# Depthwise convolution: the running sum kept in a PSUM bank instead of SBUF

## The chip, the core and the metric

The kernel runs on one core of a Trainium2 chip. The metric is the device time of one execution in microseconds (us), the median of several runs. A core has a matmul engine (PE, with its own weight-load queue PEld), a vector engine (DVE), an activation engine (ACT), a general engine (POOL), DMA queues (SP issues most of them), the on-chip memory SBUF and the accumulator memory PSUM in eight banks, one of which holds 128 partitions of 512 float32 numbers. Each engine works through its instructions in program order; an instruction that waits holds back all that stand behind it on its engine.

## What is computed

Two transformer blocks follow each other on 512 tokens of width 1024. The change lies in the first one, whose first half is this (cut):

```python
h = rmsnorm(x, norm1_g)
z = h @ w_in                                # conv_in 2048, q 1024, k 256, v 256, two gates of 1024
u = conv_in[..., :1024] * sigmoid(conv_in[..., 1024:])
u = depthwise_conv(u, dw_w, kernel=31, padding=15) + dw_b      # each of 1024 channels by itself
conv_out = silu(layernorm(u)) @ w_pw
attn_out = windowed_gqa(q, k, v, sink) @ w_o                   # 16 heads, window of 128
merged = sigmoid(g0) * conv_out + sigmoid(g1) * attn_out
x = x + merged @ w_out
x = x + peer_ffn(rmsnorm(x))                                   # experts, the long middle part
```

The second block (a recurrence, two attentions, a merge) and the last norm follow.

## The kernel before

Channels lie on the partitions. `u` is a tile of 8 blocks of 128 channels with 542 columns (512 tokens and 15 columns of padding on either side), `acc` one of 8 blocks of 512 columns; both are in SBUF.

The first stage, `mix1_in`, does the following, in the order in which the program writes it. For each of the 8 channel blocks, two projections (`mm_t`) and their product give `u` (the product is POOL's, L439). Then the values `v`. Then a pass of attention (`attn1`) over the first half of the heads and the 8 projections of the first gate; then the second pass, the convolution (`conv`, L524) with the sums for its layer norm (`conv_rms`, L534), and the 8 projections of the second gate. Then the attention's output is split in a high and a low part (`oh` by ACT, L339, `ol` by DVE, L340) and goes through `w_o`; `conv_norm` finishes the convolution; `w_pw` and `w_out` follow.

Every product of float32 matrices is made as three matmuls on their high and low parts (`mm3`, L322 to L324). One `mm_t` is 24 such matmuls into one bank named `ps`, and it needs one slab of weights: a DMA, a copy by ACT (`whi`, L316) and a subtraction of two SBUF tiles on POOL (`wlo`, L317). Slabs have two buffers. A pass of attention first projects the keys (ACT copies them, L575 and L576, DVE makes their low part, L578) and four query blocks (L586, L587), and then goes over four windows: logits (PE, L618), mask and maximum (DVE, L620), exponential (ACT, L627), division (DVE, L634), transposes (PE, L641) that DVE and ACT copy out (L643), and the product with the values (PE, L645).

The convolution of one block is one instruction at L528, `acc = u[0:512] * w[0] + bias`, and 30 at L531, `acc = u[j:j+512] * w[j] + acc`, all on DVE, 248 in all. Each reads what the one before it of the same block wrote, and so waits for it. `conv_rms` sums the eight blocks (L542), takes the mean over channels with a matmul of ones into the bank `pm` (L543), subtracts it from each block (L545), squares (ACT, L547), sums (L549), multiplies by ones again (L550) and makes the reciprocal root (L551, ACT at L1052 and L1053, DVE at L356 to L358).

PSUM has four banks `ps`, three `pa` (attention) and one `pm` in this stage. A scheduler in the build sets the order on each engine from its own estimates, the dependences and the buffers that are free; the program's order is only its starting point. It has put the convolution among the attention's instructions on DVE.

Of the kernel before, what the change touches and what calls it, by code (L numbers as in the profile page):

```python
# [15 lines left out]
OP = mybir.AluOpType  # L16
# [73 lines left out]
def _layout(inp):  # L90
# [5 lines left out]
    hp = _head_perm()  # L96
    hcol = (hp[:, :, None] * 64 + np.arange(64)).reshape(8, 128)
    arr["w1t"] = _tslabs(w, np.concatenate([conv, 2048 + hcol, _blocks(3072, 3328), _blocks(3584, 5632)]))
    arr["w1v"] = _mslabs(w[:, 3328:3584], 256, 4)
    arr["w_pw"] = _tslabs(f["conv_w_pw"][0], _blocks(0, 1024))  # L100
# [139 lines left out]
class Kern:  # L240
# [283 lines left out]
    def conv(self, u, acc):  # L524
        nc, C = self.nc, self.const
        for b in range(8):
            w = C["dw_w"][:, b * 31:(b + 1) * 31]
            nc.vector.tensor_scalar(acc[:, b, :], u[:, b, 0:512], w[:, 0:1], C["dw_b"][:, b:b + 1],  # L528
                                    op0=OP.mult, op1=OP.add)
            for j in range(1, 31):  # L530
                nc.vector.scalar_tensor_tensor(acc[:, b, :], u[:, b, j:j + 512], w[:, j:j + 1], acc[:, b, :],  # L531
                                               op0=OP.mult, op1=OP.add)

    def conv_rms(self, acc, room, kp):  # L534

# [918 lines left out]
```

## Time and profile before

| | us |
|---|---|
| median of three runs | 2652.63 (2636.78, 2652.63, 2659.26) |
| profiled execution | 2650.43 |
| its span | 2648.7 |
| PE busy | 2300.6 (87%) |
| DVE busy | 1839.5 (69%) |
| ACT busy | 838.3 (32%) |
| POOL busy | 738.1 (28%) |
| mean granted TensorE clock | 0.937 |

The span is the stretch from the first to the last instruction in the profile; the time of the execution has 1.7 us more around it. Busy time is an average over very different stages. What the change touches lies in the first 425 us: the convolution's instructions start at 38.4 us and end at 346 us. A row of the trace names the engine, the source line, the operation, and the tiles as output<-inputs.

### The profile page before, as it was taken

The numbers are of one execution on the slowest core, as the hardware profiler recorded it, in microseconds if no ns is written. First come the engines' busy times: TensorE is split into PE (matmuls) and PEld (weight loads), VectorE is DVE, ScalarE is ACT, GpSimd is POOL, SyncE is SP. The second block draws the span as 40 slices with busy tenths as digits, with TensorE's granted clock in tenths as the row PEclk, the third lists the DMA queues.
The fourth block names the chain that finished last, engine by engine and source line by source line (L and its number), as shares of the span: only waits on it lengthen the run. The fifth ranks groups of instructions, "written<-read, shape, count | busy, mean of one in ns | idle before, by whom it ended". The sixth has DMA issues, their size and how long they took to land. (4 is left out here: it accounts for less than half of the span.)

```text
span 2648.7 us, 31665 instructions
## 1 busy us (share of the span) xinstructions
PE 2300.6 (87%) x11682; PEld 1671.9 (63%) x11682; DVE 1839.5 (69%) x3541; ACT 838.3 (32%) x1781; POOL 738.1 (28%) x443
## 2 busy tenths in 40 slices
PE   7938899989989948678867868999789999999999
PEld 6826667868877725445544545663266788768887
DVE  7999975549998867575746656767767666675333
ACT  4214355333236711111111111111153433554321
POOL 4512313223126933343433433434110000000000
PEclk9969999989999979889978989999989999999999
DMA  4201113332457799998989989999731010121323
GB/s 169 96 32 45 59 48 127 120 98 81 171 203 262 256 374 387 404 412 336 415 342 390 410 350 405 408 416 417 323 115 41 25 33 27 56 88 64 104 96 120
DMA packets 142523, 551.16 MB, mean 208 GB/s; under 512 B 12704, under 2 KB 47392, under 8 KB 107040
## 3 DMA queue, kind: packets, MB, share of 16 engines
q1 hardware_dynamic: 105504, 280.69, 29.9%
q0 software_dynamic: 36864, 268.45, 25.1%
q8 instruction: 92, 1.51, 0.2%
q14 instruction: 63, 0.52, 0.1%
HBM read 524.97 MB, written 24.12 MB: 207 GB/s over the span
## 5 line engine op out<-in xcount | busy, mean ns | idle before, releaser
L192 POOL DMA_INDIRECT uv<-uv,ge x256 | 388.8, 1519 | 650.6 <-DVE x L230 576.6
L818 PE MATMUL ps<-hd,u 128*128 128x256 f32 x2048 | 463.5, 381 | 0.0
L818 PEld LDWEIGHTS ps<-hd,u 128*128 128x128 f32 x2048 | 387.1, 192 | 69.9 <-issue 20.0
L230 DVE SCALAR_TENSOR_TENSOR x<-uv,s,x 128x1024 f32<-128x1024 f32 x256 | 328.7, 1284 | 118.7 <-ACT s L222 118.4
L322 PE MATMUL ps<-hh,whi 128*128 128x512 f32 x920 | 370.8, 403 | 42.9 <-ACT whi L316 39.1
L324 PE MATMUL ps<-hh,wlo 128*128 128x512 f32 x920 | 370.9, 403 | 1.2 <-POOL wlo L317 1.2
L323 PE MATMUL ps<-hl,whi 128*128 128x512 f32 x920 | 371.1, 403 | 0.0
L317 POOL TENSOR_TENSOR wlo<-wraw,whi 128x1024 fp32r<-128x1024 f32 x84 | 214.1, 2550 | 505.8 <-ACT whi L316 472.0
L848 PE MATMUL pv<-v,ah 128*128 128x512 f32 x512 | 239.0, 623 | 110.6 <-DMA v<-v 97.1
L219 DVE CUSTOM_DVE_ANT_0 uv<-uv,rows 128x1024 f32<-128x1024 f32 x256 | 317.8, 1241 | 20.5 <-DMA uv<-uv,ge 20.4
L848 PE MATMUL pv<-v,al 128*128 128x512 f32 x512 | 240.9, 622 | 86.3 <-DMA v<-v 65.5
L316 ACT ACTIVATE whi<-wraw 128x1024 fp32r<-128x1024 f32 x151 | 159.8, 1058 | 330.8 <-PE ps L323 239.5
L848 PEld LDWEIGHTS pv<-v,ah 128*128 128x128 f32 x512 | 101.1, 200 | 236.8 <-issue 192.1
L221 ACT ACTIVATE s<-s 128x1 f32<-128x1 f32 x256 | 51.7, 202 | 602.0 <-DVE s L219 601.9
L848 PEld LDWEIGHTS pv<-v,al 128*128 128x128 f32 x512 | 99.7, 199 | 214.7 <-issue 154.1
L322 PEld LDWEIGHTS ps<-hh,whi 128*128 128x128 f32 x920 | 177.0, 192 | 81.3 <-ACT whi L316 39.5
L531 DVE SCALAR_TENSOR_TENSOR acc<-u,cols,acc 128x512 f32<-128x512 f32 x240 | 225.3, 991 | 1.0
L324 PEld LDWEIGHTS ps<-hh,wlo 128*128 128x128 f32 x920 | 176.9, 192 | 39.2 <-issue 2.0
L323 PEld LDWEIGHTS ps<-hl,whi 128*128 128x128 f32 x920 | 176.8, 192 | 39.0 <-issue 4.2
L317 DVE TENSOR_TENSOR wlo<-wraw,whi 128x1024 fp32r<-128x1024 f32 x67 | 81.9, 1223 | 113.2 <-ACT whi L316 112.8
L775 POOL TENSOR_SCALAR B<-colsp,ijw 128x128 f32<-128x128 f32 x64 | 110.9, 1740 | 50.9 <-ACT ijw L764 50.1
L840 DVE TENSOR_TENSOR ah<-ah,cg 128x256 f32<-128x256 f32 x64 | 24.9, 420 | 102.0 <-ACT ah L820 81.9
(489 smaller groups left out, 3403.1 us busy)
## 6 DMA issues: line engine op xcount, KB each, us to landing
u<-u SPq DMA_DIRECT2D x128, 512.0 KB, 8.9
v<-v SPq DMA_DIRECT2D x128, 512.0 KB, 12.5
wraw<-w2t SPq DMA_DIRECT2D x49, 512.0 KB, 3.5
wraw<-w1t SPq DMA_DIRECT2D x42, 512.0 KB, 3.5
gates<-cs SPq DMA_DIRECT2D x16, 1024.0 KB, 7.9
cg<-gates SPq DMA_DIRECT2D x16, 1024.0 KB, 36.0
wraw<-w_out SPq DMA_DIRECT2D x16, 512.0 KB, 3.5
wraw<-w_q SPq DMA_DIRECT2D x16, 512.0 KB, 3.6
```

The source lines that it names most:

```text
L192: self.k.nc.gpsimd.indirect_dma_start(t, None, self.k.ap["uv"], bass.IndirectOffsetOnAxis(ap=self.e[g][:, s:s + 1], axis=0))
L219: nc.vector.tensor_tensor_reduce(out=u, in0=u, in1=self.rows[:, g, :], scale=1.0, scalar=0.0, op0=OP.mult, op1=OP.add, accum_out=d)
L230: self.k.nc.vector.scalar_tensor_tensor(x, t[:, 1024:2048], c, x, op0=OP.mult, op1=OP.add)
L316: nc.scalar.activation(hi, raw, AF.Copy)
L317: (nc.gpsimd if self.low else nc.vector).tensor_tensor(lo, raw, hi.bitcast(F32), op=OP.subtract)
L322: mm(out, ah, bh, start=start, stop=False)
L323: mm(out, ah, bl, start=False, stop=False)
L324: mm(out, al, bh, start=False, stop=stop)
L531: nc.vector.scalar_tensor_tensor(acc[:, b, :], u[:, b, j:j + 512], w[:, j:j + 1], acc[:, b, :], op0=OP.mult, op1=OP.add)
L775: (nc.vector if n < self.near else nc.gpsimd).tensor_scalar(B[:, n, :], C["iota"], ijw[:, 1, t0 + n:t0 + n + 1], ijw[:, 2, t0 + n:t0 + n + 1],
L818: nc.tensor.matmul(ps[:, i * 256:i * 256 + 256], raw[:, k * 128:k * 128 + 128], h[:, k, :], start=k == 0, stop=k == KC - 1)
L848: nc.tensor.matmul(po[t][half], a[:, ts], v[:, half * 512:half * 512 + 512], start=j + i == 0, stop=j + i == 127)
```

## The change

The running sum of each block is kept in a tile `part` of the bank `pm`. The first instruction and those of j = 1 to 29 write there, and the last one, j = 30, reads `part` and writes `acc` in SBUF as before. There is one such bank, so a block's sum can start only when the block before it has ended.

```diff
         for b in range(8):
             w = C["dw_w"][:, b * 31:(b + 1) * 31]
-            nc.vector.tensor_scalar(acc[:, b, :], u[:, b, 0:512], w[:, 0:1], C["dw_b"][:, b:b + 1],
+            part = self.bank("pm")
+            nc.vector.tensor_scalar(part, u[:, b, 0:512], w[:, 0:1], C["dw_b"][:, b:b + 1],
                                     op0=OP.mult, op1=OP.add)
             for j in range(1, 31):
-                nc.vector.scalar_tensor_tensor(acc[:, b, :], u[:, b, j:j + 512], w[:, j:j + 1], acc[:, b, :],
-                                               op0=OP.mult, op1=OP.add)
+                nc.vector.scalar_tensor_tensor(acc[:, b, :] if j == 30 else part, u[:, b, j:j + 512], w[:, j:j + 1],
+                                               part, op0=OP.mult, op1=OP.add)
```

The scheduler answers with another order on DVE, ACT and PE up to the projection `w_o`; behind it every engine's order is as before, and POOL's is the same throughout. In the changed kernel lines behind 527 have numbers higher by one (L531 is L532 there).

On DVE, the start of the convolution before, behind its first L528, up to the first low part of the keys:

```order
L531 SCALAR_TENSOR_TENSOR acc<-u,cols,acc 128x512 x13
L528 TENSOR_SCALAR acc<-u,cols 128x512
L531 SCALAR_TENSOR_TENSOR acc<-u,cols,acc 128x512 x34
L528 TENSOR_SCALAR acc<-u,cols 128x512
L531 SCALAR_TENSOR_TENSOR acc<-u,cols,acc 128x512 x26
L528 TENSOR_SCALAR acc<-u,cols 128x512
L531 SCALAR_TENSOR_TENSOR acc<-u,cols,acc 128x512 x34
L528 TENSOR_SCALAR acc<-u,cols 128x512
L531 SCALAR_TENSOR_TENSOR acc<-u,cols,acc 128x512 x26
L528 TENSOR_SCALAR acc<-u,cols 128x512
L531 SCALAR_TENSOR_TENSOR acc<-u,cols,acc 128x512 x3
L578 TENSOR_TENSOR k<-ps,k 64x512 x2
```

Thirteen instructions belong to block 0 alone; from the second L528 on, two blocks alternate (13 and 34 are the 30 of block 0 and 17 of block 1). In the changed kernel, behind two blocks of 1, 29 and 1 instructions that stand just like the first rows here:

```order
L529 TENSOR_SCALAR pm<-u,cols 128x512
L543 TENSOR_TENSOR u<-acc 128x512
L532 SCALAR_TENSOR_TENSOR pm<-u,cols,pm 128x512 x29
L532 SCALAR_TENSOR_TENSOR acc<-u,cols,pm 128x512
L529 TENSOR_SCALAR pm<-u,cols 128x512
L543 TENSOR_TENSOR u<-u,acc 128x512
L532 SCALAR_TENSOR_TENSOR pm<-u,cols,pm 128x512 x19
L579 TENSOR_TENSOR k<-ps,k 64x512 x2
L532 SCALAR_TENSOR_TENSOR pm<-u,cols,pm 128x512 x2
L579 TENSOR_TENSOR k<-ps,k 64x512 x2
```

The blocks follow each other, and 113 of the 248 instructions stand ahead of the keys instead of 142.

On DVE, the end of the second attention pass before, up to the low part of the attention's output:

```order
L634 TENSOR_SCALAR lg<-lg,s_2388 128x256 x4
L643 COPY pT<-pa 128x512
L340 TENSOR_TENSOR meml<-memT,memh 128x2048
L356 SCALAR_TENSOR_TENSOR u<-pT 128x512
L357 TENSOR_TENSOR u<-u 128x512
L358 SCALAR_TENSOR_TENSOR pT<-u,pT 128x512
L340 TENSOR_TENSOR ol<-o,oh 128x512 x8
```

Now the convolution's last 47 instructions stand among those of this pass, and its last two behind the pass's last copy (L644 now); then come the last L543, four L546, and this:

```order
L550 TENSOR_TENSOR u<-u 128x512
L546 TENSOR_TENSOR acc<-acc,pm 128x512
L550 TENSOR_TENSOR u<-u 128x512 x3
L552 TENSOR_SCALAR u<-pm 128x512
L356 SCALAR_TENSOR_TENSOR u<-pT 128x512
L357 TENSOR_TENSOR u<-u 128x512
L358 SCALAR_TENSOR_TENSOR pT<-u,pT 128x512
L340 TENSOR_TENSOR ol<-o,oh 128x512 x8
```

All of the layer norm's sums have moved from among the attention's windows to behind them, ahead of `ol`.

On PE, the same place before; the rows of the second gate's projection repeat nine times more until `w_o` begins with `oh`:

```order
L645 MATMUL pa<-pT,v 64x512
L641 MATMUL pa<-ident,lg 128x128 x4
L645 MATMUL pa<-pT,v 64x512 x2
L323 MATMUL ps<-hl,whi 128x512
L324 MATMUL ps<-hh,wlo 128x512
L322 MATMUL ps<-hh,whi 128x512
```

And now:

```order
L646 MATMUL pa<-pT,v 64x512
L642 MATMUL pa<-ident,lg 128x128 x4
L646 MATMUL pa<-pT,v 64x512 x2
L544 MATMUL pm<-u,ones 128x512
L551 MATMUL pm<-u,ones 128x512
L323 MATMUL ps<-ol,whi 128x512
L324 MATMUL ps<-oh,wlo 128x512
L322 MATMUL ps<-oh,whi 128x512
```

The gate's projections stand ahead of the last window's end, and behind it PE has nothing but the two matmuls of ones and `w_o`.

## Rows read from the trace of the kernel before

**Rows 1.** By stretch: length, busy PE, PEld, DVE, ACT, POOL (count); clock, DMA share, GB/s.
```profile
38.40:175.70 137.30, 101.79 (x501) 85.72 (x499) 136.78 (x142) 29.21 (x41) 55.76 (x25) 0.88 0.23 77
175.70:204.50 28.80, 19.19 (x62) 14.48 (x62) 28.32 (x31) 9.46 (x13) 9.50 (x4) 0.68 0.20 62
204.50:302.20 97.70, 89.17 (x396) 61.95 (x397) 92.35 (x206) 43.73 (x107) 24.24 (x9) 0.97 0.14 47
302.20:335.60 33.40, 24.64 (x110) 20.27 (x109) 32.56 (x41) 10.18 (x14) 11.92 (x5) 0.93 0.23 79
335.60:421.80 86.20, 83.42 (x365) 55.29 (x365) 65.72 (x163) 53.26 (x123) 17.29 (x8) 0.99 0.15 49
```

**Rows 2.** Busy time by stretch of line L531 alone: length, DVE busy (count), clock, DMA.
```profile
38.40:175.70 137.30, 132.19 (x136) 0.88 0.23 77
204.50:302.20 97.70, 48.74 (x64) 0.97 0.14 47
302.20:335.60 33.40, 19.19 (x15) 0.93 0.23 79
```

**Rows 3.** Timeline of DVE in the convolution: start us, us, engine, line, operation, count.
```profile
43.40 2.33 DVE L531 SCALAR_TENSOR_TENSOR acc<-u,cols,acc 128x512 f32<-128x512 f32 x3
...
51.83 2.77 DVE L531 SCALAR_TENSOR_TENSOR acc<-u,cols,acc 128x512 f32<-128x512 f32 x1
...
155.92 17.31 DVE L531 SCALAR_TENSOR_TENSOR acc<-u,cols,acc 128x512 f32<-128x512 f32 x26
```

**Rows 4.** Timeline of POOL.
```profile
51.28 2.77 POOL L317 TENSOR_TENSOR wlo<-wraw,whi 128x1024 fp32r<-128x1024 f32 x1 [0.82 <-ACT whi L316]
...
179.34 2.35 POOL L317 TENSOR_TENSOR wlo<-wraw,whi 128x1024 fp32r<-128x1024 f32 x1 [46.61 <-ACT whi L316]
```

**Rows 5.** Timeline of ACT where keys and queries begin; brackets: idle before, releaser.
```profile
130.76 0.59 ACT L576 ACTIVATE k<-ps 64x512 fp32r<-64x512 f32 x1
177.12 0.59 ACT L575 ACTIVATE k<-ps 64x512 fp32r<-64x512 f32 x1 [45.77 <-DVE k L578]
...
178.22 1.04 ACT L316 ACTIVATE whi<-wraw 128x1024 fp32r<-128x1024 f32 x1
```

**Rows 6.** Timeline of PE at the same place.
```profile
179.32 0.80 PE L322 MATMUL ps<-hh,whi 128*128 128x512 f32 x1 [39.10 <-ACT whi L316]
```

**Rows 7.** DVE lines one by one: count: nanoseconds min/median/max, first and last start.
```profile
L531 DVE SCALAR_TENSOR_TENSOR acc<-u,cols,acc x240: 711/744/2947, 39.0 to 345.4; 128x512 f32<-128x512 f32 x120
...
L587 DVE SCALAR_TENSOR_TENSOR q<-ps,q x16: 685/689/695, 182.9 to 334.9; 64x512 fp32r<-64x512 f32 x16
...
L545 DVE TENSOR_TENSOR acc<-acc,pm x8: 656/680/686, 348.1 to 364.8; 128x512 f32<-128x512 f32 x8
...
L542 DVE TENSOR_TENSOR u<-u,acc x6: 676/678/693, 315.0 to 346.2; 128x512 f32<-128x512 f32 x6
```

**Rows 8.** The page's costliest groups: busy us, mean ns, idle before, releaser.
```profile
L230 DVE SCALAR_TENSOR_TENSOR x<-uv,s,x 128x1024 f32<-128x1024 f32 x256 | 328.7, 1284 | 118.7 <-ACT s L222 118.4
```

**Rows 9.** Timeline of DVE in the norm's sums, the last copies and `w_o`.
```profile
372.49 0.69 DVE L551 TENSOR_SCALAR u<-pm 128x512 f32<-128x512 f32 x1 [1.62 <-PE pm L550]
...
408.84 0.69 DVE L643 COPY pT<-pa 128x512 f32<-128x512 f32 x1 [1.72 <-PE pa L641]
...
413.26 0.69 DVE L356 SCALAR_TENSOR_TENSOR u<-pT 128x512 f32<-128x512 f32 x1 [1.53 <-ACT pT L1053]
...
415.44 9.32 DVE L340 TENSOR_TENSOR ol<-o,oh 128x512 fp32r<-128x512 f32 x8
...
465.56 0.69 DVE L463 SCALAR_TENSOR_TENSOR gate<-gate,ps 128x512 f32<-128x512 f32 x1 [4.86 <-PE ps L324]
```

**Rows 10.** Timeline of ACT in the same stretch.
```profile
372.24 1.28 ACT L1052 ACT_TABLE_LOAD   x1
373.53 0.63 ACT L1052 ACTIVATE u<-u 128x512 f32<-128x512 f32 x1
...
413.86 0.60 ACT L600 ACTIVATE o<-pa 128x512 f32<-128x512 f32 x1 [0.63 <-PE pa L645]
```

## The prediction

> **What bounds the kernel now.** Behind `w_o` nothing is reordered, so the change is decided in the first 421 us. I set that end by the first gate product that waits for nothing but its own matmuls: the eighth at 465.6 us, 4.86 + 0.69 = 5.55 us behind the seventh [rows 9]; eight times 5.55 before it is 421 us, where PE begins `w_o`. From there on PE is the engine that the stage waits for, and what PE gains or loses until then moves everything later by as much.
>
> I read the stretches first [rows 1]. From 38.4 to 175.7 us DVE is busy 136.8 of 137.3 us, with the convolution alone [rows 2], and PE only 101.8. The timeline says why. ACT has copied the first keys at 131.35 us and then stands idle for 45.8 us for DVE's L578 [rows 5]; the next slab's `whi` waits behind it on ACT, and PE without that slab for 39.1 us, until 179.3 [rows 6]. DVE isn't waiting for anything then: its order has 142 instructions of the convolution ahead of L578, and it is still working through them. So here DVE is the bound. [...] In the windows of the first pass both engines are near full (PE 89.2 of 97.7, DVE 92.4); in the second pass's projections DVE is (32.6 of 33.4); in its windows PE is (83.4 of 86.2), and DVE has 20 us to spare.
>
> Then what one L531 costs. Three that depend on each other take 2.33 us [rows 3]: 0.75 for one and (2.33 - 0.75) / 2 = **0.79 us** from start to start. Where two blocks alternate, 26 take 17.31 us: (17.31 - 0.74) / 25 = **0.66 us**. So waiting for the instruction directly before costs 0.13. But in the first stretch 136 of them take 132.2 us [rows 2], 0.97 each; over all 240 the median is 0.744 and the maximum 2.947 [rows 7]. The long ones are blocked: the one at 51.83 us lasts 2.77 and ends just after POOL's subtraction of 51.28, which lasts 2.77 too [rows 3, 4]. L587 is an instruction of the same kind with one input in PSUM and one in SBUF, and of its 16 none took over 0.695 us [rows 7], though POOL was busy 9.5 of the 28.8 us of the stretch in which the first of them ran [rows 1]. I read this so: DVE and POOL block each other only where DVE takes two tensors from SBUF, and the changed L531 takes one.
>
> **The change, part by part.** It takes away the blocking, it takes away the alternation (one bank), and it adds a write to PSUM.
>
> *Price of one instruction, p.* No row shows DVE writing to PSUM. Reading it is free: L545, with one input in PSUM, has a median of 0.680 us and L542, all SBUF, 0.678 [rows 7]. The lower bound is 0.66, the pipelined price; a chain can't go below it unless the write is faster than any here. For the upper bound I pay the fixed part of an instruction once more: 1024 columns take 1.284 us [rows 8], 512 take 0.744, so a column takes 1.05 ns and the fixed part is 0.744 - 0.540 = 0.20; 0.79 + 0.20 = 1.0. I take **0.79**, the chained price in SBUF, since the read side shows no difference; behind another instruction 0.66, so 0.75 where others stand between. [...]
>
> *Up to the keys.* Ahead of L578 now stand 109 L531, 4 L528 and 2 L542: 109 x 0.79 + 4 x 0.69 (L551 in rows 9, one input and a scalar) + 2 x 0.68 = 90 us. DVE is there at 128.5; the keys are there at 131.4. L578 so starts at 131.4 instead of 175.7. The chain from there: two L578 1.4, ACT's two copies 1.1 and `whi` 1.0 [rows 5], POOL 2.35 [rows 4], 137.3 us. PE needs the slab at 179.3 - 39.1 = 140.2. The 39.1 us are gone, with 3 to spare; p up to (134.3 - 38.4 - 4.2) / 109 = 0.84 costs nothing here.
>
> *Queries.* PE goes on with the two query blocks left (48 of the 62 matmuls in rows 1), 2 x 5.55 us at full clock, to 151.3, and the first masks can start at about 153 instead of 204.5. DVE has 17 instructions of the convolution, four L578, six L587 (0.69 each) and an L542 in the same time: 17 x 0.79 + 10 x 0.69 + 0.7 = 21 us, to 152.4. **Gain 51**: the wait, and 12 us of half clock and full DVE.
>
> *First windows.* DVE: 92.4 - 48.7 for the rest [rows 1, 2], and 54 x 0.75 + 0.7, is 85 us; PE: 89.2 at 0.97 is 86.5 at full clock. PE waited 8.5 us here; I leave it 5.5. 92 us instead of 97.7: **gain 5**, at 245 us.
>
> *Second projections.* PE 24.6 x 0.93 = 23, DVE 17 x 0.75 + 12 x 0.69 + 0.7 = 22: 24 instead of 33.4 us. **Gain 9**, at 269.
>
> *Second windows.* Here the change costs. 47 of the convolution's instructions now stand where DVE had room: 43.7 + 47 x 0.75 + 3 (an L542 and `meml`) = 82 us on DVE beside PE's 83, as in the first windows. I take 90 instead of 85.4: **loss 5**, at 359.
>
> *Behind the last window.* DVE goes straight from the last copy through two L531 (1.6), L542 (0.7), two matmuls of ones with their waits (2 x 1.6 [rows 9]), fifteen L545 and L549 (15 x 0.68 = 10.2), L551 (0.7), ACT's two operations and one table load that nothing hides (2 x 0.63 + 1.28 [rows 10], 0.3 for handing over), L356 to L358 (415.44 - 413.26 = 2.2) and the first `ol` (9.32 / 8 = 1.2): 22.6 us. PE's own rest after that copy takes about 5 (408.84 to 413.86 before [rows 9, 10]). So PE stands 18 us, where it had the gate's projections before. Then eight `ol` at 1.2 feed the first block of `w_o`: 9.4 us instead of 5.55, 4 more; and after such an idle time the clock was low for part of the next stretch: 3, an estimate from the 0.68 in rows 1. **Loss 25**: `w_o` starts at 384.
>
> Sum: 421 - 384 = 37 us, 1.4%. The profiled execution took 2650.4, 2 us under the median of its three runs: **2613 us**.
>
> **Rivals.**
>
> *PSUM is slow to write (slower).* A chained instruction must wait until the bank has taken all; if the fixed part is paid again on the write and on the read, p = 0.79 + 2 x 0.2 = 1.2. DVE then reaches L578 at 38.4 + 109 x 1.2 + 5 = 174, as late as before, projections and windows are DVE's: queries 17 x 1.2 + 8 = 28, first windows 43.7 + 54 x 1.17 + 6 = 113, second projections 29, second windows 47 + 47 x 1.17 + 6 = 108, behind them 26: 478, 57 us late, 2707. At p = 1.0 the same sum gives 38.4 + 114 = 152 for L578, 175 for the masks, then 101, 25, 97 and 26: 424, no gain. So it decides from 1.0 on. For it: that no row shows such a write. Against it: the read, which shows nothing. 6%.
>
> *POOL goes on blocking (same).* If what collides is `u` with POOL's reads, and not the second SBUF tensor, L531 stays chained and blocked. Up to the keys 132.2 - 136 x 0.744 = 31 us are blocked time now; most of it falls in the first 90 us. L578 at 157, masks at 181 (half clock again), then 92, 33, 92, 25: 423, 2652. Against it: 16 L587 without one blocked. 8%.
>
> *The tail eats more (same).* If the second windows are slowed by DVE as much as the first ones were (97.7 for 89.2) and PE's clock stays low for longer, the second windows take 96 and the end 33: 398, 2627. For it: DVE's load there rises from 66 to 82 of 86 us. 14%.
>
> That the sum doesn't go to PSUM is excluded by the order of instructions, where 29 of 30 write `pm`.
>
> **Numbers.** Forecast 72%. With p = 0.66 the windows would take 89 and 86 and the time is 2606; the runs shown lie 22 us apart, so some 10 to either side. Low end 2592; the high end takes in the tail and prices up to 0.95: 2645. What a measurement can tell from no change is 1%, 26.5 us: faster means under 2626, slower over 2679. Faster: 72%. Same: 8 + 14 - 1 = 21%. Slower: 6% and 1% for the unforeseen, 7%.
>
> **What the profile of the changed kernel would show.** L532 with a median near 0.75 us and no long ones; 113 instructions of the convolution up to the keys in about 90 us and ACT's wait for L579 under 5 us; PE's wait for `whi` of 39 us gone and the clock in that stretch near 1.0; a new wait of PE of 15 to 20 us for the matmul of ones and `ol`, with a low clock behind it; DVE busy down by about 45 us. A median of L532 over 0.95 proves the price wrong, durations of 2 to 3 us prove the blocking wrong, and a second-window stretch over 96 us proves me wrong on who has room there.

## The result, and the profile after

The changed kernel takes **2603.6 us** (median of six runs, 2585.8 to 2617.4), the kernel before 2650.7 in the same comparison: a ratio of 0.983, 95% interval 0.981 to 0.986. Timed twice more beside other kernels, the ratio was 0.982 both times (0.979 to 0.985, and 0.978 to 0.986). The forecast was 2613 with a range of 2592 to 2645. The profiled execution took 2607.0 us, its span is 2605.2 and its mean clock 0.945; that is 43.5 us less than the one before.

From the page: busy time by engine, and the convolution's group (busy us, mean ns, idle time before it).

```profile
PE 2293.5 (88%) x11682; PEld 1665.3 (64%) x11682; DVE 1791.3 (69%) x3541; ACT 839.3 (32%) x1781; POOL 719.2 (28%) x443
...
L532 DVE SCALAR_TENSOR_TENSOR pm<-u,cols,pm 128x512 f32<-128x512 f32 x232 | 174.5, 752 | 5.4
```

DVE is busy 48 us less; 45 of that are the convolution's steps (busy 225.3 us before, 180.5 now). Its instructions one by one (count: nanoseconds min/median/max):

```profile
L529 DVE TENSOR_SCALAR pm<-u,cols x8: 801/814/816, 38.4 to 300.7; 128x512 f32<-128x512 f32 x8
L532 DVE SCALAR_TENSOR_TENSOR pm<-u,cols,pm x232: 717/756/757, 39.3 to 354.8; 128x512 f32<-128x512 f32 x116
L532 DVE SCALAR_TENSOR_TENSOR acc<-u,cols,pm x8: 733/748/749, 62.2 to 355.6; 128x512 f32<-128x512 f32 x8
```

L529 and L532 are L528 and L531 of before. The durations of the 240 steps added up to 237.8 us before (where two blocks alternate, they overlap); 35 took over 0.9 us and up to 2.947 [rows 7], 60 us more than as many at the median. Each of the 35 ended 0.54 to 0.55 us behind an instruction of POOL, 28 behind a subtraction of L317 and 7 behind a product of L439. Now the 240 add up to 180.5 us and the longest takes 0.757, although 107 of them overlap an instruction of POOL. DVE's timeline ahead of the keys (start us, us, line, count):

```profile
99.34 12.63 DVE L532 SCALAR_TENSOR_TENSOR pm<-u,cols,pm 128x512 f32<-128x512 f32 x16
112.00 0.75 DVE L532 SCALAR_TENSOR_TENSOR acc<-u,cols,pm 128x512 f32<-128x512 f32 x1
...
113.58 2.41 DVE L543 TENSOR_TENSOR u<-u,acc 128x512 f32<-128x512 f32 x1
115.92 12.62 DVE L532 SCALAR_TENSOR_TENSOR pm<-u,cols,pm 128x512 f32<-128x512 f32 x16
...
131.34 1.38 DVE L579 TENSOR_TENSOR k<-ps,k 64x512 fp32r<-64x512 f32 x2 [0.43 <-ACT k L577]
```

And POOL's, beside these and in the tail:

```profile
107.61 2.40 POOL L317 TENSOR_TENSOR wlo<-wraw,whi 128x1024 fp32r<-128x1024 f32 x1 [1.98 <-ACT whi L316]
113.05 2.39 POOL L317 TENSOR_TENSOR wlo<-wraw,whi 128x1024 fp32r<-128x1024 f32 x1 [3.04 <-ACT whi L316]
...
119.31 2.41 POOL L317 TENSOR_TENSOR wlo<-wraw,whi 128x1024 fp32r<-128x1024 f32 x1 [2.15 <-ACT whi L316]
...
349.81 2.35 POOL L317 TENSOR_TENSOR wlo<-wraw,whi 128x1024 fp32r<-128x1024 f32 x1 [4.62 <-ACT whi L316]
385.38 2.60 POOL L317 TENSOR_TENSOR wlo<-wraw,whi 128x1024 fp32r<-128x1024 f32 x1 [33.22 <-ACT whi L316]
```

Sixteen steps in a row take 12.63 us, (12.63 - 0.75) / 15 = 0.79 from start to start, whatever POOL does meanwhile. L543 between them takes two tensors from SBUF, and it is blocked: 2.41 us instead of 0.68, ending 0.55 us behind POOL's subtraction of 113.05. Both kinds stand side by side here. L579 now starts at 131.34 us instead of 175.7. So ACT's wait of 45.77 [rows 5] has become 1.45, and PE's wait of 39.1 for the next slab [rows 6] is gone. ACT at the keys:

```profile
132.76 0.59 ACT L576 ACTIVATE k<-ps 64x512 fp32r<-64x512 f32 x1 [1.45 <-DVE k L579]
```

By stretch, cut where the changed kernel's own stages lie (columns as in rows 1):

```profile
38.40:131.30 92.90, 92.87 (x463) 78.66 (x462) 88.37 (x115) 29.20 (x41) 48.05 (x24) 1.00 0.32 108
131.30:155.00 23.70, 23.70 (x111) 19.53 (x110) 22.50 (x36) 11.22 (x16) 11.16 (x5) 1.00 0.27 90
155.00:246.90 91.90, 86.38 (x389) 59.09 (x388) 80.73 (x188) 42.33 (x106) 20.36 (x9) 1.00 0.16 52
246.90:271.00 24.10, 24.10 (x112) 19.97 (x111) 23.31 (x38) 10.18 (x14) 10.96 (x5) 1.00 0.27 89
271.00:359.00 88.00, 78.19 (x356) 52.29 (x354) 78.63 (x183) 45.68 (x111) 19.15 (x8) 1.00 0.20 66
359.00:378.60 19.60, 4.48 (x8) 2.43 (x9) 14.49 (x24) 10.05 (x13) 0.00 (x0) 0.56 0.00 0
```

In the first five PE runs at full clock, where it had 0.88 and 0.68 before [rows 1]. The price stands in the sixth: for 19.6 us PE is nearly empty and its granted clock 0.56. PE there (in brackets the idle time before, and what ended it):

```profile
357.14 1.13 PE L544 MATMUL pm<-u,ones 128*128 128x512 f32 x2 [1.09 <-DVE u L543]
...
367.83 2.08 PE L551 MATMUL pm<-u,ones 128*128 128x512 f32 x2 [9.57 <-DVE u L550]
...
376.19 0.80 PE L323 MATMUL ps<-ol,whi 128*128 128x512 f32 x1 [6.29 <-DVE ol L340]
376.79 0.63 PE L324 MATMUL ps<-oh,wlo 128*128 128x512 f32 x1
```

DVE from the last copy on:

```profile
354.24 0.68 DVE L644 COPY pT<-pa 128x512 f32<-128x512 f32 x1
...
369.94 0.69 DVE L552 TENSOR_SCALAR u<-pm 128x512 f32<-128x512 f32 x1 [2.17 <-PE pm L551]
373.27 0.69 DVE L356 SCALAR_TENSOR_TENSOR u<-pT 128x512 f32<-128x512 f32 x1 [2.64 <-ACT pT L1054]
...
375.45 4.90 DVE L340 TENSOR_TENSOR ol<-o,oh 128x512 fp32r<-128x512 f32 x8
...
423.20 0.69 DVE L463 SCALAR_TENSOR_TENSOR gate<-gate,ps 128x512 f32<-128x512 f32 x1 [4.89 <-PE ps L324]
```

PE waits 1.1, 9.6 and 6.3 us for DVE. The first matmuls of `w_o` then start every 0.43 us, at a granted clock of 0.50 up to 381.9, where later ones start every 0.23. (Of the seven sums over the blocks, L543, only the last stands behind the windows; the other six stand among the steps of the convolution.)

The eighth gate product, by which the prediction set the end of the changed part, is the mark from here on. It starts at 423.20 instead of 465.56 [rows 9]: 42.4 us. The other 1.1 us of the 43.5 lie behind it. In two more profiles of the changed kernel it started at 429.1 and 430.8. There the clock was 0.87 in the first 38 us, ahead of the change, where it was 1.00 here and before, and the convolution's first instruction started at 41.7 and 41.6 us instead of 38.4. Counted from that instruction to the mark, the gain is 42 us in the first profile and 40 and 38 in these two. What lies behind the mark (2171 to 2183 us in these four profiles, 2155 to 2191 in all thirteen of this document) varies by as much as small changes are worth; the experiments are therefore read at the mark too. By the medians the gain is 45 to 47 us. Where the few us beyond the 38 to 42 come from is not shown.

Of the control with one bank below, one execution at a granted clock of 0.83, where the others had 0.94, is left out.

### The profile page after: what moved, and what is told of

The parts are those of the page before. It is cut to its first block, busy times and chain, and to the rows that moved or that the text cites. A ratio compares the mean times of both kernels' runs of the same rounds, so it can differ in the third digit from the quotient of the medians.

```text
span 2605.2 us, 31677 instructions
## 1 busy us (share of the span) xinstructions
PE 2293.5 (88%) x11682; PEld 1665.3 (64%) x11682; DVE 1791.3 (69%) x3541; ACT 839.3 (32%) x1781; POOL 719.2 (28%) x443
## 5 line engine op out<-in xcount | busy, mean ns | idle before, releaser
L192 POOL DMA_INDIRECT uv<-uv,ge x256 | 382.2, 1493 | 659.6 <-DVE x L230 579.3
L317 POOL TENSOR_TENSOR wlo<-wraw,whi 128x1024 fp32r<-128x1024 f32 x84 | 205.0, 2441 | 473.3 <-ACT whi L316 452.5
L532 DVE SCALAR_TENSOR_TENSOR pm<-u,cols,pm 128x512 f32<-128x512 f32 x232 | 174.5, 752 | 5.4
L317 DVE TENSOR_TENSOR wlo<-wraw,whi 128x1024 fp32r<-128x1024 f32 x67 | 81.9, 1222 | 112.4 <-ACT whi L316 112.0
```

The source lines that it names most:

```text
L192: self.k.nc.gpsimd.indirect_dma_start(t, None, self.k.ap["uv"], bass.IndirectOffsetOnAxis(ap=self.e[g][:, s:s + 1], axis=0))
L317: (nc.gpsimd if self.low else nc.vector).tensor_tensor(lo, raw, hi.bitcast(F32), op=OP.subtract)
L532: nc.vector.scalar_tensor_tensor(acc[:, b, :] if j == 30 else part, u[:, b, j:j + 512], w[:, j:j + 1], part, op0=OP.mult, op1=OP.add)
```

## Experiments

Three theories of the gain: **blocking** (DVE and POOL hold each other up where DVE takes two tensors from SBUF; PSUM takes one of them away), **order** (one chain after the other, and not the place of the sum), and **traffic** (long steps come from DMA or PE).

**The same chain in SBUF.** The sum takes one block of `acc` instead of the bank:

```diff
-            part = self.bank("pm")
+            part = acc[:, 7, :]
```

> The running sum stays one chain, as in the changed kernel, but in a block of SBUF, so that each step takes two tensors from SBUF again. Theory (POOL blocks a step with two SBUF tensors): of the 232 steps some 30 take over 0.9 us, up to 2.9; the 123 convolution instructions ahead of the keys' L579 last 123 x 0.79 + about 28 of blocked time, so L579 stands at 160 to 170 us and not at 131; ACT's wait there is 30 us or more; time 2635 to 2660. Rival (the gain came from the order, with one block after the other, and not from PSUM): no more long steps than the changed kernel has, L579 at about 138, time 2600 to 2615.

Measured: 2650.5 us, a ratio of 1.002 (1.000 to 1.004). The steps one by one:

```profile
L532 DVE SCALAR_TENSOR_TENSOR acc<-u,cols,acc x240: 732/752/2919, 38.9 to 387.9; 128x512 f32<-128x512 f32 x120
```

A run of seventeen of them on DVE's timeline:

```profile
54.54 23.34 DVE L532 SCALAR_TENSOR_TENSOR acc<-u,cols,acc 128x512 f32<-128x512 f32 x17
```

ACT at the keys:

```profile
177.31 0.59 ACT L576 ACTIVATE k<-ps 64x512 fp32r<-64x512 f32 x1 [46.02 <-DVE k L579]
```

Again 35 steps last over 0.9 us. Seventeen take 23.34 us, 1.4 each instead of 0.79; the wait for the keys is back with 46.0 us. Nothing of the gain is left, so it comes from PSUM. I had put L579 at 160 to 170 us, with 28 us of blocked time ahead of it; the blocked time was 40 us, and L579 came at 175.9. A chain pays for both, 0.79 a step and the blocks.

**The two sides apart.** Odd steps read SBUF and write PSUM, even ones read PSUM and write SBUF:

```diff
-                nc.vector.scalar_tensor_tensor(acc[:, b, :] if j == 30 else part, u[:, b, j:j + 512], w[:, j:j + 1],
-                                               part, op0=OP.mult, op1=OP.add)
+                into, of = (part, acc[:, b, :]) if j % 2 else (acc[:, b, :], part)
+                nc.vector.scalar_tensor_tensor(into, u[:, b, j:j + 512], w[:, j:j + 1], of, op0=OP.mult, op1=OP.add)
```

(The block's first instruction, L529, writes `acc` again.)

> The sum passes to and fro: odd steps read it from SBUF and write it to PSUM, even steps read it from PSUM and write it to SBUF. Theory (what counts is the second input tensor in SBUF): of the 120 odd steps some 15 take 2 to 2.9 us, of the 120 even ones none over 0.9; about half the blocked time of before, some 20 us, comes back, mostly ahead of the keys, so L579 at 140 to 150 and the time 2615 to 2635. Rival A (the output's side decides): the even ones are long and the odd ones not. Rival B (any PSUM operand frees the instruction): neither kind is long and the time is that of the changed kernel, 2604. On the price of a write both kinds should have a median near 0.75; a dearer write would show in the odd ones alone.

Measured: 2632.2 us, ratio 0.995 (0.993 to 0.997). The block's first step, the odd and the even ones:

```profile
L529 DVE TENSOR_SCALAR acc<-u,cols x8: 534/543/2318, 38.3 to 143.4; 128x512 f32<-128x512 f32 x8
L533 DVE SCALAR_TENSOR_TENSOR pm<-u,cols,acc x120: 724/760/2934, 38.9 to 370.7; 128x512 f32<-128x512 f32 x120
L533 DVE SCALAR_TENSOR_TENSOR acc<-u,cols,pm x120: 707/748/750, 39.6 to 372.0; 128x512 f32<-128x512 f32 x120
```

The even steps never take over 0.750 us, although 40 of them overlap an instruction of POOL. Of the odd ones 28 last over 0.9 us, up to 2.934: more than the 15 expected, with 41 us of blocked time. So the second input decides here (0 of 120 long steps against 28 of 120), and an output in PSUM does not free a step that takes two tensors from SBUF. L579 comes at 159.6 us, later than the 140 to 150 forecast, because more were blocked.

**POOL's work taken away.** The kernel before, with POOL's subtractions in this stage made by DVE:

```diff
-            self.low = True
             r = self.mix1_in(xp, kp)
-            self.low = False
```

(and the same in `mix1_in` around `project_out`)

> The kernel before, with POOL's subtraction of the weights' low parts given to DVE in this stage; the convolution's sum stays in SBUF. Theory: the long steps go with POOL's work; of the 240 at most 8 or so, beside POOL's eight products of L439, still take over 0.9 us, against 35. Rival (the long steps come from SBUF traffic that the DMA queues or PE cause): 25 or more stay long. DVE has some 40 subtractions of 1.1 to 1.3 us more to do, so the time tells nothing here and may be above 2650.

One execution took 2638.3 us. The steps, whose line is L528 in this kernel:

```profile
L528 DVE SCALAR_TENSOR_TENSOR acc<-u,cols,acc x240: 714/743/1791, 39.4 to 365.2; 128x512 f32<-128x512 f32 x120
```

Five steps are over 0.9 us, none over 1.8, each beside one of POOL's products of L439 (L438 in this kernel). With that, traffic as a cause falls: DMA, PE and the sum in SBUF are all still there. The keys' low part came at 140.3 us instead of 175.7, although DVE had POOL's work as well.

Then the tail. Why does PE stand 18 us there, and what does it cost? **Work put into the gap:**

```diff
-                ps = self.mm_t(w1t[26 + 8 * p + b], h)
+                ps = self.mm_t(w1t[26 + 8 * p + b], h, ps=self.pa() if p and b >= 5 else None)
```

> The last three projections of the second gate take their bank from the windows' pool, so PE has 71 of their 72 matmuls around the two matmuls of ones, where it stood 18 us. Theory (the tail costs because PE has nothing to do there): PE's idle time between the last window and the first block of the output projection falls from 18 to under 5 us, the half clock there is gone (worth 3 us), the windows ahead get up to 9 us shorter (DVE is busy 78.6 of their 88), but POOL splits weights meanwhile, so the eight ol take 1.1 to 1.2 us again and not 0.6; time 2590 to 2600. Rival (DVE's chain sets the end of the windows and of the tail whatever PE does): the output projection starts within 2 us of where it did, time 2600 to 2606.

Measured: 2608.0 us beside 2601.1 of the changed kernel; the ratios to before overlap (0.982 to 0.988, and 0.979 to 0.985). In its profile the keys come when they came in the first profile of the changed kernel (131.4 and 131.3 us), and the mark is 7.2 us later, at 430.4; counted from the convolution's first instruction, it is 3 and 4 us later than in the other two. DVE's timeline in the tail:

```profile
351.77 0.69 DVE L644 COPY pT<-pa 128x512 f32<-128x512 f32 x1 [0.33 <-PE pa L642]
...
359.99 2.48 DVE L546 TENSOR_TENSOR acc<-acc,pm 128x512 f32<-128x512 f32 x4 [3.77 <-PE pm L544]
...
363.59 2.40 DVE L550 TENSOR_TENSOR u<-u 128x512 f32<-128x512 f32 x1
...
380.27 1.00 DVE L356 SCALAR_TENSOR_TENSOR u<-pT 128x512 f32<-128x512 f32 x1 [5.12 <-ACT pT L1054]
...
382.76 4.91 DVE L340 TENSOR_TENSOR ol<-o,oh 128x512 fp32r<-128x512 f32 x8
```

POOL beside it:

```profile
363.03 2.42 POOL L317 TENSOR_TENSOR wlo<-wraw,whi 128x1024 fp32r<-128x1024 f32 x1 [40.16 <-ACT whi L316]
```

And ACT:

```profile
377.24 1.06 ACT L316 ACTIVATE whi<-wraw 128x1024 fp32r<-128x1024 f32 x1 [1.43 <-PE pa L323]
378.31 1.28 ACT L1054 ACT_TABLE_LOAD   x1
```

The gap was half filled (PE waits 8 us for DVE there instead of 17) and nothing was won: the rival's reason holds, and the time is no better, if not worse. The last copy is only 2.5 us earlier, and the first matmuls of `w_o` start every 0.43 us here too, from 384.1 to 388.4. From the copy on the norm on DVE is the path, and the filling slows it: L546 waits 3.8 us for the matmul of ones that now stands behind others on PE, L550 is blocked by POOL (2.40 instead of 0.68, and 4.32 us for three), and the root waits while ACT works on a slab and loads its table (5.1 us). One guess failed: the eight `ol` took 4.9 us here too, since none of POOL's subtractions fell on them.

**Two banks.** The sum alternates between two banks, and the windows have two instead of three; the control has two for the windows and one for the sum:

```diff
-            with k.banks(ps=4, pa=3, pm=1) as k.pp:
+            with k.banks(ps=4, pa=2, pm=2) as k.pp:
```

> Two banks for the sum, one fewer for the windows: two blocks alternate again, in PSUM. The price of a step falls from 0.79 to 0.66 us start to start; 128 instructions ahead of the keys instead of 113. Theory (the lost alternation costs nothing up to the keys, where PE sets the pace, but DVE has 10 to 20 us more room behind them, and the norm's sums move back among the windows, with the gate's projections behind): no idle time of 9 us for the second matmul of ones; time 2580 to 2600. Rival (two banks for the windows slow PE by more than that): the two stretches of windows take over 95 us each and the time is 2605 or more.

> Control to the two banks: one bank for the sum as in the changed kernel, and also one fewer for the windows. Tells apart what the alternation gives from what the order gives that comes with two window banks (here too the first matmul of ones stands ahead of the last window, and 92 of the gate's matmuls behind the second). Theory: the tail's idle time goes here as well, so 2585 to 2602, and the kernel with two banks is 0 to 10 us faster than this one. Rival (windows with two banks cost more than the tail): 2605 to 2625.

Measured: 2611.9 and 2629.4 us, beside 2601.1. The norm's sums moved among the windows (in the control in part), and still the rivals' reason holds in both; the control is above even the 2605 to 2625 of its rival. The second windows, from the first mask to the last copy (columns as in rows 1), in the changed kernel:

```profile
267.30:354.20 86.90, 79.68 (x368) 54.75 (x367) 78.68 (x187) 44.29 (x109) 21.56 (x9) 1.00 0.20 65
```

With two banks for either:

```profile
275.60:382.30 106.70, 92.85 (x377) 58.88 (x377) 80.59 (x188) 51.31 (x119) 22.29 (x9) 0.94 0.17 56
```

And in the control:

```profile
274.00:388.80 114.80, 95.28 (x373) 60.20 (x373) 93.97 (x205) 48.01 (x116) 21.48 (x9) 0.90 0.16 52
```

They take 107 and 115 us instead of 87. A bank of the windows was worth more than the tail. Between the two, alternation gives some 18 us of time, more than the 0 to 10 I had thought.

**Three and two.** So the second bank is taken from the projections:

```diff
-            with k.banks(ps=4, pa=3, pm=1) as k.pp:
+            with k.banks(ps=3, pa=3, pm=2) as k.pp:
```

**The output split ahead of the norm.** `ol` lies in the buffer of `u`, where the norm had its working blocks too, and so waited for its end. The norm gets blocks of the keys' buffer, and everything behind its first matmul moves behind the split:

```diff
-                r = self.conv_rms(acc, [u[:, b, 0:512] for b in range(8)], kp)
+                rest = self.conv_rms(acc, u[:, 0, 0:512], kp)
...
             self.split(oh[b], ol[:, b, :], o[:, b, :])
+        r = rest()
...
+            room = kp.tile([128, 4, 512], F32, name="sums", tag="kv")
```

> Two banks for the sum and three for the windows; a projection's bank is given up for it. Theory: alternation at 0.66 a step frees DVE 20 us and the norm ends among the windows, with some 118 of the gate's matmuls behind them, while the windows keep their pace of 87 us (with two banks they took 107); time 2580 to 2595. Rival (projections with three banks wait for their evictions): PE waits between blocks of the projections, time 2600 or more.

> The norm's squares get room in the keys' buffer, so the low parts ol, which take the place of the convolution's input, no longer wait for the norm; they are split ahead of it, and the norm runs beside the output projection. Theory (the tail costs because the output projection waits for DVE's whole norm through ol, not because PE is empty): the first block starts 15 to 18 us earlier, PE's idle time behind the last window falls from 18 to under 4 us, the half clock goes, and the time is 2578 to 2590. Rival (the norm is only put off, and the next projection waits for it, since POOL's splits block its steps with two SBUF tensors): a new wait of 10 us or more of PE for hl, time 2595 to 2605.

> Both at once: two banks for the sum, three for the projections, and ol ahead of the norm. Theory: if the two gains come from the same 18 us, the time is that of the better of the two, 2575 to 2590; if the alternation also shortens the windows, 2565 to 2575. Rival: as of the other two, 2595 or more.

| kernel | median us | ratio to before (95%) | mark at | from the convolution's first instruction |
|---|---|---|---|---|
| changed, the same comparison | 2600.2 | 0.982 (0.978 to 0.986) | 429.1 | 387.5 |
| three and two | 2595.8 | 0.981 (0.978 to 0.984) | 412.0 | 372.4 |
| `ol` ahead of the norm | 2587.9 | 0.979 (0.977 to 0.982) | 409.1 | 368.1 |
| both | **2578.2** | 0.976 (0.972 to 0.979) | 403.3 | 363.7 |

In the first, DVE's steps alternate, twenty-five at (16.55 - 0.75) / 24 = 0.66 us each:

```profile
99.51 16.55 DVE L532 SCALAR_TENSOR_TENSOR pm<-u,cols,pm 128x512 f32<-128x512 f32 x25
```

Its second windows keep their pace with three banks, 84 us:

```profile
270.80:355.20 84.40, 80.61 (x368) 54.74 (x367) 75.49 (x189) 48.88 (x116) 19.80 (x8) 1.00 0.18 58
```

The rival expected PE to wait between blocks of the projections. It does, but little: from 38.4 to 131.3 us PE is busy 91.4 of 92.9 us, where the changed kernel has 92.9, and the keys come 95.0 us behind the convolution's first instruction instead of 92.9.

In the second, DVE begins to split `ol` 4 us behind the last copy, and the norm goes on beside `w_o`:

```profile
355.68 0.68 DVE L652 COPY pT<-pa 128x512 f32<-128x512 f32 x1
...
359.98 4.91 DVE L340 TENSOR_TENSOR ol<-o,oh 128x512 fp32r<-128x512 f32 x8 [2.24 <-PE pm L545]
...
367.80 2.48 DVE L556 TENSOR_TENSOR sums<-sums 128x512 f32<-128x512 f32 x1
...
409.13 0.69 DVE L464 SCALAR_TENSOR_TENSOR gate<-gate,ps 128x512 f32<-128x512 f32 x1 [1.51 <-PE ps L324]
```

PE waits 0.8 us for `ol` instead of 6.3:

```profile
360.73 0.50 PE L323 MATMUL ps<-ol,whi 128*128 128x512 f32 x1 [0.78 <-DVE ol L340]
...
378.75 1.12 PE L557 MATMUL pm<-sums,ones 128*128 128x512 f32 x2 [2.20 <-DVE sums L556]
```

So PE's idle time was a matter of what `ol` waits for, not of PE having no work. With both, PE has no gap at all in the stretch in which it stood (columns as in rows 1):

```profile
271.00:359.00 88.00, 84.14 (x380) 56.64 (x379) 77.41 (x190) 46.91 (x118) 20.16 (x8) 1.00 0.15 49
359.00:378.60 19.60, 19.60 (x85) 15.46 (x84) 15.11 (x19) 15.37 (x20) 9.37 (x4) 1.00 0.67 242
```

The last column takes out that the clock in the first 38 us was 0.87 in the first and third of these profiles and 1.00 in the others. By it the two are 15 and 19 us ahead, and both together 24: partly the same gain. (The three profiles of the changed kernel lie between 384.8 and 389.2.) By their medians alone the first two can't be told from the changed kernel, since the intervals overlap; for both together the intervals just touch. That version is the fastest of all: 22 us below the changed kernel, 67 below the one before.

## Why the prediction was right, point by point

- **Price of a step, 0.79:** right, 0.79 from start to start. Chained in SBUF the median step is 0.752 us, chained in PSUM 0.756. So the sum in PSUM costs the median step 4 ns more.
- **Blocking gone:** right, and shown by the odd and even steps. The row that it leaned on was thin: of the 16 L587 only 5 overlapped an instruction of POOL. And the rule was put too narrowly. L529, as in the kernel with the sides apart, takes one tensor only, from SBUF to SBUF, and was blocked as well (2.318 us); with its output in PSUM it took at most 0.816.
- **Keys at 131.4, masks at 153, second projections from 245, done at 269:** measured 131.34, 151.96, 246.9 and 270.2. The gain of 51 us up to the masks was 52.6. What the half clock has of it no run shows by itself; the granted clock before was 0.50 from 179.3 to 187 us, 0.99 up to 197.5 and 0.50 again from 198 to 204.5, and in the changed kernel it was 1.00 from 131.3 to 155.
- **Second windows slower, to 359:** PE ends the last window and the first matmul of ones there; the stretch took 88 us and not 90, from 271. DVE did fill up, with 78.6 of 88 us.
- **Behind the last window, loss 25:** this term was too large, and in one part of it. From the last copy to the first matmul that waits for `ol` I had 22.6 us; it was 22.0 (354.24 to 376.19). The clock cost 3, as estimated: the matmuls from 376.2 to 381.9 ran at half speed (a granted clock of 0.50, one every 0.43 us instead of 0.23), 5.7 / 2 = 2.9. But the feeding of the first block by eight `ol` at 1.2 us, 4 us, cost nothing. They took 0.6 each. I had carried over the 9.32 us of before [rows 9], which were blocked time; in the changed kernel POOL has no slab to subtract while PE stands: its rows go from 349.81 to 385.38. So `w_o` starts, by the same reckoning, at 423.2 - 44.4 = 378.8 and not 384.
- **Sum:** 37 us forecast to this point; 42.4 in this profile, and 40 and 38 in the two others, counted from the convolution's first instruction. Against the profiled execution of 2607.0 the forecast of 2613 was 6 us high: 5 are the term above, and 1 lies behind the mark. Against the median of 2603.6 it was 9 us high.
- **Rivals:** the slow write and the blocking by POOL's reads are refuted by the rows of L532 (median 0.756 us, none over 0.757). The larger tail is too; it was smaller than forecast.

## What to carry to other kernels

Before moving a running sum, look whether its long instructions are blocked ones: take the spread of one line's durations, not its mean, and lay another engine's timeline beside it. Where two SBUF tensors collided with POOL, a second input in PSUM (not the output) was enough here: no step of 120 over 0.750 us, against 28 of 120 over 0.9 with the output there. And when an engine stands idle behind a move, ask first what its next operand waits for: half filling the gap with work gained nothing (3 to 7 us later at the mark), while freeing the one buffer gained 19.

## What the runs showed that was not expected

- A write to PSUM costs the two-tensor step next to nothing (median 0.760 us into PSUM, 0.752 into SBUF, both with two inputs in SBUF), but not the single-tensor one: L529 took 0.814 us into PSUM and 0.543 into SBUF. At eight instructions it is 2 us. Why the two kinds differ is not shown.
- The alternation that the change gave up was worth some 18 us, where the second window bank was held fixed (2629.4 against 2611.9), although a step differs by 0.13 us only, 240 x 0.13 = 31 us if all were on the path.
- POOL is held up as well. In the run without its subtractions its eight products of L439, all of one shape, took between 1.09 and 5.29 us. The three long ones, 3.9 to 5.3 us, ran beside back-to-back steps on DVE and ended 1.0 to 1.2 us behind a subtraction that DVE made between them. But one of 1.48 us ran beside such steps as well, so what decides is not shown.
